# Channel shuffle: the tiles at both ends of a load-copy-store pipeline become larger

## The chip, the cores and the metric

One core of one Trainium2 chip runs the kernel. The metric is the time of one execution on the device in microseconds (us), taken as the median of several runs. A profile, recorded in one execution, is read beside it.

A few words that recur: VectorE (DVE in the profile) is the engine that copies here. SP and ACT are the engines whose sequencers issue transfers; the work of a transfer is done by 16 DMA engines that the core has. The on-chip memory has 128 partitions, and "38 KB a partition" means 128 rows of 38 KB.

## The reference

The input is a tensor of 16 x 64 x 64 x 256 values in float32, 67.11 MB. Its 256 channels are seen as 8 groups of 32, and the two are swapped: channel `g*32 + j` goes to place `j*8 + g`.

```python
def reference(x, groups):
    batch, h, w, c = x.shape
    channels_per_group = c // groups
    x = x.reshape(batch, h, w, groups, channels_per_group)
    x = x.transpose(0, 1, 2, 4, 3)
    x = x.reshape(batch, h, w, c)
    return x.astype(np.float32)
```

No arithmetic is done. Every byte is read once and written once.

## The kernel before

There are 65,536 pixels of 256 channels (1 KB each), 512 pixels for each partition. The list `_SLOTS` cuts these 512 into tiles, in order: the numbers are pixels, and so KB, a partition. A tile of several numbers is loaded, copied and stored in so many parts. Before, the list is a tile in two parts (4 and 8), one of 28, twelve of 38 and one of 16.

The loop over `_SLOTS` (L45) takes a load buffer (`in_tile`, L46) and a store buffer (`out_tile`, L47). Both have the size of the largest tile, 38 KB a partition; there are two load buffers and three store buffers, used in turn. For each part of a tile it issues three things:

- a load on SP's queue (L55): DRAM to `in_tile`. A part is one contiguous block of DRAM; each partition gets one contiguous row of it.
- a copy on VectorE (L57): `in_tile` to `out_tile`, and this copy carries out the shuffle through its access pattern.
- a store on ACT's queue (L61): `out_tile` to DRAM, again one contiguous row for a partition.

What orders the work: instructions on one engine run in the order in which they are written. A load into a buffer waits until the copy of the tile two places earlier is done. A copy waits for its load and, from the fourth tile on, for the store of the tile three places earlier. A store waits for its copy. SP issues nothing but loads and ACT nothing but stores, so neither holds the other up. No scheduler reorders anything (`manual_schedule`).

Transfers of one issuing engine are worked off in order by the DMA engines. Loads and stores are separate queues on the same 16 DMA engines.

Of the kernel before, what the change touches and what calls it, by code (L numbers as in the profile page):

```python
# [1 line left out]

# [4 lines left out]


F32 = mybir.dt.float32
P = 128  # L10

_SLOTS = [[4, 8], [28]] + [[38]] * 12 + [[16]]
_IN_BUFS = 2
_OUT_BUFS = 3


@with_exitstack
def kernel(
    ctx: ExitStack,
    tc: tile.TileContext,  # L20
    x: bass.AP,
    groups: bass.AP,
    out: bass.AP,
):
    nc = tc.nc
    b, h, w, c = x.shape
    G = int(groups)
    CPG = c // G
    assert G * CPG == c
    assert sum(map(sum, _SLOTS)) * P == b * h * w  # L30
    biggest = max(map(sum, _SLOTS))

    x_flat = x.rearrange("b h w c -> (b h w c)")
    out_flat = out.rearrange("b h w c -> (b h w c)")

    in_pool = ctx.enter_context(tc.tile_pool(name="in_pool", bufs=_IN_BUFS))
    out_pool = ctx.enter_context(tc.tile_pool(name="out_pool", bufs=_OUT_BUFS))

    def rows(flat, first, q):

        return flat[first * c : (first + P * q) * c].rearrange("(p f) -> p f", p=P)

    ctx.enter_context(tc.manual_schedule(engines=None))
    first = 0
    for parts in _SLOTS:  # L45
        in_tile = in_pool.tile([P, biggest * c], F32, name="in_tile")  # L46
        out_tile = out_pool.tile([P, biggest * c], F32, name="out_tile")  # L47
        at = 0
        pieces = []
        for q in parts:  # L50
            pieces.append((q, first, slice(at * c, (at + q) * c)))
            first += P * q
            at += q
        for q, start, cols in pieces:
            nc.sync.dma_start(out=in_tile[:, cols], in_=rows(x_flat, start, q))  # L55
        for q, start, cols in pieces:
            nc.vector.tensor_copy(  # L57
                out=out_tile[:, cols].rearrange("p (i j g) -> p i j g", j=CPG, g=G),
                in_=in_tile[:, cols].rearrange("p (i g j) -> p i j g", g=G, j=CPG),
            )  # L60
            nc.scalar.dma_start(  # L61
                out=rows(out_flat, start, q), in_=out_tile[:, cols]
            )


# [1 line left out]
_INS = ['x', 'groups']  # L67
_OUTS = [((16, 64, 64, 256), 'float32')]

_NUMBERS = {'groups': 8}  # L70


# [26 lines left out]
```

## Time and profile before

| what | value |
|---|---|
| time, median of 3 runs | 316.34 us (316.31 to 316.68) |
| span of the profiled execution, first to last instruction | 314.4 us |
| what lies between the span and the median | 1.9 us |
| DMA traffic | 67.11 MB read, 67.11 MB written |
| mean rate over the span | 427 GB/s |
| load of 38 KB a partition, issue to landing (median of 12) | 37.0 us |
| store of 38 KB a partition, issue to landing (median of 12) | 42.6 us |
| last load (16 KB), issue to landing | 30.4 us |
| last store (16 KB), issue to landing | 15.2 us |
| first store (4 KB), issue to landing | 14.3 us |

The profile gives no time of its own for the profiled execution beyond its span; the sums are made against the span, and the rest up to the median is taken as it stands.

How to read it: the page begins with the span and the busy time of each engine. "DMA queues" then lists packets, bytes and the share that the packets took of the time of all 16 DMA engines; a share of 50% in a window of 100 us means 800 us of packet time, spread over 16 engines. The queue view can be asked for any window; it counts the packets that start inside it, so a short window can show more than 100%. The load queue is q1, the store queue q10. In a group line such as those of the copies, the columns are: line, engine, operation, output and input, their shapes, the count; then busy us and the mean ns of one; then the idle time of the engine before them and what ended it. In a timeline line the first two numbers are start and duration in us.

### The profile page before, as it was taken

The numbers are of one execution on the slowest core, as the hardware profiler recorded it, in microseconds if no ns is written. First come the engines' busy times: TensorE is split into PE (matmuls) and PEld (weight loads), VectorE is DVE, ScalarE is ACT, GpSimd is POOL, SyncE is SP. The second block draws the span as 40 slices with busy tenths as digits, with TensorE's granted clock in tenths as the row PEclk, the third lists the DMA queues.
The fourth block names the chain that finished last, engine by engine and source line by source line (L and its number), as shares of the span: only waits on it lengthen the run. The fifth ranks groups of instructions, "written<-read, shape, count | busy, mean of one in ns | idle before, by whom it ended". The sixth has DMA issues, their size and how long they took to land.

```text
span 314.4 us, 132 instructions
## 1 busy us (share of the span) xinstructions
DVE 119.0 (38%) x16; POOL 0.2 (0%) x4
## 2 busy tenths in 40 slices
DVE  2081907309109109019028028037046055065400
POOL 0000000000000000000000000000000000000000
DMA  7999999999999999999999999999999999999997
GB/s 317 405 441 416 435 416 483 401 465 406 450 421 446 426 436 436 401 470 396 475 396 475 396 470 401 470 401 470 401 450 421 446 426 436 436 417 450 429 421 321
DMA packets 4608, 134.22 MB, mean 427 GB/s; under 512 B 512, under 2 KB 512, under 8 KB 768
## 3 DMA queue, kind: packets, MB, share of 16 engines
q1 hardware_dynamic: 2304, 67.11, 49.8%
q10 hardware_dynamic: 2304, 67.11, 49.4%
HBM read 67.11 MB, written 67.11 MB: 427 GB/s over the span
## 4 chain that ended last, share of the span: by engine, by line
DMA 76%; DVE 19%; issue 0%; SPq 0%; DVEq 0%
DMA in_tile<-in_x_dram 76%; DVE out_tile L57 19%; SPq L55 0%; DVEq L57 0%
## 5 line engine op out<-in xcount | busy, mean ns | idle before, releaser
L57 DVE COPY out_tile<-in_tile 128x9728 f32<-128x9728 f32 (+4 forms) x16 | 119.0, 7440 | 179.4 <-DMA in_tile<-in_x_dram 179.4
L80 POOL MEMSET const-uint8-127<- 128x1 uint8 x1 | 0.1, 103 | 0.0
L80 POOL MEMSET const-bfloat16-1.0<- 128x1 bf16 x1 | 0.1, 102 | 0.0
L80 POOL MEMSET const-float32-1.0<- 128x1 f32 x1 | 0.1, 100 | 0.0
L80 POOL MEMSET const-float32-0.0<- 128x1 f32 x1 | 0.1, 99 | 0.2 <-issue 0.2
## 6 DMA issues: line engine op xcount, KB each, us to landing
in_tile<-in_x_dram SPq DMA_DIRECT2D x12, 4864.0 KB, 37.0
out_dram<-out_tile ACTq DMA_DIRECT2D x12, 4864.0 KB, 42.6
in_tile<-in_x_dram SPq DMA_DIRECT2D x1, 3584.0 KB, 14.7
out_dram<-out_tile ACTq DMA_DIRECT2D x1, 3584.0 KB, 30.9
in_tile<-in_x_dram SPq DMA_DIRECT2D x1, 2048.0 KB, 30.4
out_dram<-out_tile ACTq DMA_DIRECT2D x1, 2048.0 KB, 15.2
in_tile<-in_x_dram SPq DMA_DIRECT2D x1, 1024.0 KB, 5.4
out_dram<-out_tile ACTq DMA_DIRECT2D x1, 1024.0 KB, 25.0
```

The source lines that it names most:

```text
L57: nc.vector.tensor_copy(out=out_tile[:, cols].rearrange("p (i j g) -> p i j g", j=CPG, g=G), in_=in_tile[:, cols].rearrange("p (i g j) -> ...
L80: nc = _bacc.Bacc("TRN2", target_bir_lowering=False, num_devices=1)
```

## The change

One line changes. The tile in two parts (4 and 8 KB) and the tile of 28 KB at the beginning give way to one tile of 24 KB; the twelve tiles of 38 KB stay; the last tile grows from 16 to 32 KB. There are 14 tiles in place of 15, each in one part, so 14 loads, copies and stores in place of 16. The two load buffers and three store buffers and their sizes stay, as does all other code.

```diff
-_SLOTS = [[4, 8], [28]] + [[38]] * 12 + [[16]]
+_SLOTS = [[24]] + [[38]] * 12 + [[32]]
 _IN_BUFS = 2
 _OUT_BUFS = 3
```

## The prediction

> **What bounds the kernel now.** I read the page first, then the DMA view in short windows, then copies by shape, the timeline and the chain of waits. The page's head:
>
> ```profile
> span 314.4 us, 132 instructions
> DVE 119.0 (38%) x16; POOL 0.2 (0%) x4
> ...
> q1 hardware_dynamic: 2304, 67.11, 49.8%
> q10 hardware_dynamic: 2304, 67.11, 49.4%
> ```
>
> q1 carries the loads, q10 the stores. Their packets fill 99.2% of the 16 DMA engines' span; VectorE works 38% of it. The chain's 76% for loads and 19% for copies is only the order in which work ended; while VectorE sat in that chain the DMA engines were busy with stores. So the limit is DMA time, and an edit can change the end in three ways: less DMA time, a hole in it, or another start or finish.
>
> A transfer has 2304/16 = 144 packets, so 9 for each engine: 8 rows and one packet that reports completion. How the queues share an engine, from windows 80 to 264 us and 9.11 to 17.73:
>
> ```profile
> q10 hardware_dynamic: 1152, 39.85, 50.1%
> q1 hardware_dynamic: 1152, 39.85, 50.1%
> ```
>
> ```profile
> q1 hardware_dynamic: 128, 3.54, 96.3%
> q10 hardware_dynamic: 128, 0.52, 14.8%
> ```
>
> Both windows have equal counts, although in the second a store row is 4 KB and most load rows 28 KB. The queues take turns packet by packet; bytes don't count. A row's time is share x 16 x window / rows. 38 KB: 0.501 x 16 x 184 / 1024 = 1.440 us. 4 KB: 0.148 x 16 x 8.62 / 128 = 0.159. In the same way 8 KB takes 0.309 (20.25 to 31.86, 21.3%), 28 KB 1.063 (34.6 to 52.17, 48.4%) and 16 KB 0.611 (278.7 to 292.7, 34.9%).
>
> **The DMA time that the change removes and adds.** Removed: rows of 4, 8, 28 and 16 KB, 8 an engine, once in each queue: 8 x (0.159 + 0.309 + 1.063 + 0.611) = 17.14 us. Added: 24 and 32 KB rows. No row has them; between their neighbours, 0.611 + 8/12 x 0.452 = 0.912 and 1.063 + 4/10 x 0.377 = 1.214; 8 x 2.126 = 17.01. The difference, 0.13 a queue, is **-0.26 us** for two. The bounds are the best and worst bytes per second of those rows: at the 4 KB row's rate the 56 KB take 8 x 14 x 0.159 = 17.81 a queue (+1.3 for both), at the 38 KB row's 8 x 56/38 x 1.440 = 16.98 (-0.3). I keep -0.26, since both new sizes lie between rows that run near the 38 KB rate. The other twelve tiles and all bytes stay.
>
> The Trainium skill, page "DMA: Bandwidth & Descriptors", section "Anatomy of one DMA — SWDGE (gpsimd) path", counts a fixed cost of about 2.0 us for each transfer, beside the bytes. Four transfers fewer would by that rule (an estimate) save 8 us, for some 308. The packet times above contradict it for queued transfers, and I don't use it in the sum.
>
> **Issue and copy work.** Two DMA issues fewer on SP (0.33 us each) and on ACT (0.36): hidden now by rows in flight, worth nothing; without that cover they would be a gain of 2 x 0.33 + 2 x 0.36 = 1.4. VectorE loses copies of 1.09, 2.02, 6.57 and 3.87 and gains two; between the rows below, 24 KB (6144 elements) takes 3.87 + 2/3 x 2.70 = 5.67 and 32 KB (8192) 6.57 + 0.4 x 2.22 = 7.46. In total -0.4 us on an engine that idles 179, so nothing, except at the two ends.
>
> ```profile
> L57 DVE COPY out_tile<-in_tile 128x9728 f32<-128x9728 f32 x12 | 105.5, 8791 | 158.5 <-DMA in_tile<-in_x_dram 158.5
> L57 DVE COPY out_tile<-in_tile 128x7168 f32<-128x7168 f32 x1 | 6.6, 6569 | 7.7 <-DMA in_tile<-in_x_dram 7.7
> L57 DVE COPY out_tile<-in_tile 128x4096 f32<-128x4096 f32 x1 | 3.9, 3873 | 7.6 <-DMA in_tile<-in_x_dram 7.6
> ```
>
> **The start.** The first load is issued at 0.73; no packet starts before 1.74, and the windows after it are full. Both kernels have this lead of 1.02 us. The load that completes the first 12 KB landed at 6.59 = 1.75 + 8 x (0.159 + 0.309) + 1.10. So the 24 KB tile lands at 1.75 + 7.30 + 1.10 = 10.15 (the 4 KB one landed at 4.0), its copy ends at 15.84 and its store is issued at 15.87 instead of 5.19. That later first store costs nothing as long as loads fill the engines: the 38 KB load is queued behind the 24 KB one and lasts until about 9.8 + 8 x 1.44 = 21.3, and the third load is issued at 15.84. If it were not there, the cost would be the wait from 9.8 to the store.
>
> What the later store does change is how many load turns run ahead of the first store turn; call it the lead. Before, the store issued at 5.19 had its first packet at about 9.12 (the q10 rows of the window from 9.11 on). Between 6.3 and 9.11 the engines started only loads:
>
> ```profile
> q1 hardware_dynamic: 32, 0.92, 80.3%
> ```
>
> That is two 28 KB rows an engine (0.92 MB / 32), after one that began by 6.3. So the lead was 9 + 9 + 3 = 21 turns. I read it as: the store arrives 1.1 to 1.75 us after its issue, during the first 28 KB row, and two packets are already taken ahead of it. After the change the arrival is at 17.0 to 17.6. The 38 KB rows start at 9.8 + 1.44 k, so the sixth is then running (from 17.0), and two more go ahead: lead 9 + 8 = 17. If the arrival catches the fifth, or if the 3.93 us are plain delay (15.87 + 3.93 = 19.8, when seven rows are through), it is 16. I take 17 and keep 16 for the range.
>
> In the middle a lead of 17 is enough. When a load lands, 17 - 9 = 8 store turns are still queued, which alternate with loads and last about 8 x 2.88 = 23 us, against a copy of 8.8. The output buffers wait on a store three tiles back, long done; no new wait arises.
>
> **The end, where cover is thin.** After the last load nothing but queued stores keeps the DMA engines busy until the last copy is stored. Before: 144 load turns, lead 21, so 123 store turns done of the 135 up to the last 38 KB store: 12 left, of which 10 are rows, 14.4 us. The window 294.42 to 308.42, from that landing on, bears this out:
>
> ```profile
> q10 hardware_dynamic: 192, 5.87, 97.0%
> ```
>
> 192/16 = 12 packets. The last copy and store fit into it easily:
>
> ```profile
> 294.54 3.87 DVE L57 COPY out_tile<-in_tile 128x4096 f32<-128x4096 f32 x1 [7.62 <-DMA in_tile<-in_x_dram]
> ```
>
> After: 126 load turns, lead 17, 109 store turns done of 117: 8 left, 7 of them rows, **10.08 us** of cover. Needed: last row to landing 0.35 (the last store's rows end at 313.28, it lands at 298.45 + 15.2), 0.12 to the copy (294.42 to 294.54), 7.46 of copy, 0.03 to the issue, then the way to the first store packet. The trace shows no store to idle engines. The nearest row is the first load, 1.02; the other end is the first store's 3.93, rows in front of it included. I take 1.02: the need is 8.98 and 1.1 us remain. Cost of the tail: 0. With lead 16 the cover is 6 x 1.44 = 8.64 and a hole of 0.34 opens, 1.07 if the way takes 1.75.
>
> The same rule of the page (about 2.0 us, mostly the receipt) speaks against the change here, since at the tail nothing hides it. With 2.0 for the 0.35 and 1.02 the need would be 9.61: still covered with lead 17, a hole of 0.97 with 16 (an estimate from that page).
>
> **Sum.** 314.4 - 0.26 = 314.2 for the span. The three runs before have median 316.34, so 1.9 us lie around the span; I leave these as they are. 316.34 - 0.26 = **316.1 us**. A measurement of this kernel can tell about 0.2% (0.63 us) from no change, so this is no change.
>
> **Rivals.** (1) A short hole: lead 16 with 1.02 to 1.75 to the packet. 316.1 + 0.34 to 1.07 = 316.4 to 317.2. For it: the fifth row ends just where the arrival may fall. Against: before, all 16 engines agreed on three rows, which puts the arrival past 1.1 us.
> (2) Slower: the last store, issued at the tail, needs its 3.93 us even on idle engines. Need 11.89, hole 1.81 (lead 17) to 3.25 (lead 16): 317.9 to 319.3. It decides from a way of 10.08 - 7.96 = 2.1 us on. For it: that is the only store start in the trace. Against: whole 28 KB rows passed in that time, 3.2 us of it, so queued packets explain it.
> (3) Faster: the small rows cost more than their packet time. Packets ran from 1.75 to 313.28, 311.5 us; all 512 KB a partition and queue at the 38 KB rate need 16 x 512/38 x 1.440 = 310.4. If all of that 1.1 came from small tiles, 315.2. Against: much of it is the stream's start, which stays.
>
> **Chances.** Forecast 0.53, (1) 0.23, (2) 0.15, (3) 0.07, a loss of another kind 0.02. Over 0.2% faster: (3) and 0.01 of the forecast's edge, 0.08. Slower: (2), the rest 0.02, and 0.07 of (1) that lies above 317.0, 0.24. Same: 0.68. The forecast's own range is 315.9 to 316.4. The range to be held takes in (1), some of (3) and the foot of (2): 315.6 to 317.8.
>
> **What would show it.** Both queues' shares still near 99%, first packet near 1.75, first copy starting near 10.2, first store packet after eight 38 KB load rows an engine, last landing of a load near 295 with 7 rows of 38 KB left, and packets without a break to the end. Wrong: a stretch near 303.5 in which no packet starts, or row times off the line for 24 or 32 KB.

## The result and the profile after

The changed kernel takes 317.15 us in the median of 11 runs, the kernel before 316.31 us in 11 runs beside them. The ratio is 1.0029, with a 95% interval of 1.002 to 1.0039: 0.3% slower. Three of the eleven executions took 331.5 to 334.2 us and are left out of the ratio; none of the 11 of the kernel before did. The prediction was 316.1 us and no change. The measured time lies inside the range that was given (315.6 to 317.8), but on the other side of no change from the forecast's small gain.

The profiled execution took 316.71 us, the shortest of the eleven. The head of its page:

```profile
span 314.9 us, 121 instructions
DVE 119.5 (38%) x14; POOL 0.2 (0%) x4
...
q1 hardware_dynamic: 2016, 67.11, 49.8%
q10 hardware_dynamic: 2016, 67.11, 49.3%
```

99.1% against 99.2%: the DMA engines are as full as before, and the span is still 0.5 us longer. The difference sits in four places.

**The start.** The DMA view of the changed kernel from 1.72 to 9.63 us holds the 128 rows of the first tile:

```profile
q1 hardware_dynamic: 128, 3.15, 100.2%
```

1.002 x 16 x 7.91 / 128 = 0.991 us a row. Later rows of 24 KB take 0.912 (the store window 22.2 to 38.7: 44.2% x 16 x 16.5 / 128), as predicted. So the start costs 8 x 0.079 = 0.63 us beyond the rows. The first copy, which waits for this tile, starts at 10.73:

```profile
10.73 5.72 DVE L57 COPY out_tile<-in_tile 128x6144 f32<-128x6144 f32 x1 [10.73 <-DMA in_tile<-in_x_dram]
```

Before, the window 1.74 to 5.88 was filled in this way:

```profile
q1 hardware_dynamic: 270, 1.56, 97.9%
```

That is 4.05 us an engine. Of the 270 packets 16 report completion and 254 are rows (128 of 4 KB, 126 of 8 KB), worth 3.71: 0.34 lost.

**The row ahead of the first store.** From 19.8 to 22.2 us the 16 engines of the changed kernel start one row each, the last of the first 38 KB load:

```profile
q1 hardware_dynamic: 16, 0.62, 100.6%
```

1.006 x 16 x 2.4 / 16 = 2.41 us for a row that takes 1.44 elsewhere: 0.97 us lost on every engine, and the first store row comes behind it. Before, two rows show the same, the one ahead of the first store (7.99 to 9.1) and one before the 28 KB store began (32.9 to 34.6):

```profile
q1 hardware_dynamic: 16, 0.46, 106.0%
```

```profile
q1 hardware_dynamic: 15, 0.58, 98.8%
```

1.060 x 16 x 1.11 / 16 = 1.18 for a row of 1.063 is 0.11 lost, and 0.988 x 16 x 1.7 / 15 = 1.79 against 1.44 is 0.35. Smaller lengthenings stand between these two in the kernel before, 0.10 in 9.11 to 17.73 (96.3% is 132.8 us over 16 engines, for rows worth 131.2) and, in the same way, 0.14 in 20.25 to 31.86. Together 0.70. The stretches beside these windows hold 0.11 more (5.88 to 7.99, 17.73 to 20.25, 31.86 to 32.9), and 9.63 to 19.8 in the changed kernel holds 0.04: 0.81 before, 1.01 after.

**The tail.** After the last load lands, at 294.24 us, the stores of the changed kernel run on, in the windows 294.24 to 303.5 and 303.5 to 313.2:

```profile
q10 hardware_dynamic: 96, 3.74, 93.2%
```

```profile
q10 hardware_dynamic: 146, 4.19, 100.2%
```

Six 38 KB rows an engine start after the landing and a seventh is running, and then the 32 KB rows follow without a break. The last copy ends in time:

```profile
294.32 7.55 DVE L57 COPY out_tile<-in_tile 128x8192 f32<-128x8192 f32 x1 [12.27 <-DMA in_tile<-in_x_dram]
```

Its store is issued at 301.89 and the first of its rows starts at about 303.5, behind the rows of the store before. No hole opened at the tail in this execution.

**After the last landing.** SP's waits at the end of the program, for the kernel before and then for the changed one (us in total, times, longest):

```profile
SPq L94 <- DMA out_dram<-out_tile: 49.1, 3, 33.0
```

```profile
SPq L94 <- DMA out_dram<-out_tile: 54.3, 1, 54.3
```

The final waits check the completion semaphores of the transfers two at a time, in a fixed order. Before, the one that came last was the last to be checked. With 14 transfers in place of 16, the last store's semaphore is in the first pair, and three more checks of about 0.065 us follow when it has come. From the last landing to the end of the program 0.985 us pass in place of 0.813: 0.17 more.

**The sum of it:** row time -0.26, start +0.29, rows ahead of the stores +0.20, final waits +0.17: +0.40. The spans differ by 0.5. About 0.1 us is not assigned; a lengthened row can overlap the start of the next, so no single term is surer than that.

### The profile page after: what moved, and what is told of

Read it like the earlier page. It is cut to its first block, busy times and chain, and to the rows that moved or that the text cites. A ratio compares the mean times of both kernels' runs of the same rounds, so it can differ in the third digit from the quotient of the medians.

```text
span 314.9 us, 121 instructions
## 1 busy us (share of the span) xinstructions
DVE 119.5 (38%) x14; POOL 0.2 (0%) x4
## 4 chain that ended last, share of the span: by engine, by line
DMA 76%; DVE 19%; issue 0%; SPq 0%; DVEq 0%
DMA in_tile<-in_x_dram 76%; DVE out_tile L57 19%; SPq L55 0%; DVEq L57 0%
## 5 line engine op out<-in xcount | busy, mean ns | idle before, releaser
L57 DVE COPY out_tile<-in_tile 128x9728 f32<-128x9728 f32 (+2 forms) x14 | 119.5, 8536 | 182.4 <-DMA in_tile<-in_x_dram 182.4
```

Of the source, the lines that this page charges most:

```text
L57: nc.vector.tensor_copy(out=out_tile[:, cols].rearrange("p (i j g) -> p i j g", j=CPG, g=G), in_=in_tile[:, cols].rearrange("p (i g j) -> ...
```

## The experiments

Each run is compared with runs of the kernel before on the same chip, 316.1 to 316.2 us in the median. STORE, HEAD, QUEUE, TAIL, START and COUNT are names of theories; where one was changed by a result, the next expectation has it in its new form. Each is put into words in the expectation that names it first.

**again.** The changed kernel without an edit.

> The changed kernel once more, for a second profiled execution. Both theories: a median near 317.1 us. Theory HEAD (the loss of 0.8 us is at the start: the first 24 KB rows start slowly, and near 20 us the last 38 KB load row ahead of the first store is stretched by about 1.0 us): these two stretches are in this profile too, with the same sizes, and the rows of the last 38 KB store run into those of the 32 KB store without a break. Theory TAIL (most executions have a hole ahead of the last store, which the first profile, of a fast execution, happened not to have): when this profile's span is longer than 314.9 us, the difference is a stretch near 303.5 us in which no packet starts.

317.40 us, ratio 1.0033 (1.0021 to 1.0046): the loss repeats. The profiled execution took 334.8 us: in it one engine falls up to 13 us behind the others, so it does not decide between HEAD and TAIL, which stayed with the next run.

**tail_halves.** The last tile in two copies and two stores, columns 0 to 16 KB and 16 to 32 KB of the same rows. In this form of the list the first sizes of a tile are those of its loads, the second those of its copies and stores.

```diff
-_SLOTS = [[24]] + [[38]] * 12 + [[32]]
+_SLOTS = [([24], [24])] + [([38], [38])] * 12 + [([32], [16, 16])]
```

> The last 32 KB tile is loaded as before but copied and stored in two halves of 16 KB a partition, so the first of its stores is issued about 3.6 us earlier and no hole can open at the tail. HEAD: 317.0 to 317.3 us, as the changed kernel, since the start is untouched and two extra row turns cost 0.1. TAIL: 316.4 to 316.7, the hole of the median execution is gone.

Ratio 1.0032 (1.0019 to 1.0045), no gain: the typical loss isn't a hole at the tail. The profiled execution took 317.11 us, close to the median of the change, and its span is 315.3, 0.9 over the kernel before. Its start, from 1.72 to 9.62:

```profile
q1 hardware_dynamic: 126, 3.10, 102.4%
```

1.027 us a row, so 0.92 over the plain 8 rows, 0.58 more than before. With -0.2 for the rows, +0.2 for the rows ahead of the stores and +0.19 for the final waits (1.007 us from the last landing to the end) that gives about +0.8 of the 0.9. This suggests that a median execution of the changed kernel differs from its shortest mostly by the start; no profile of the unedited kernel at its median shows it.

**head_parts.** The first 24 KB as blocks of 4, 8 and 12, each loaded, copied and stored by itself.

```diff
-_SLOTS = [[24]] + [[38]] * 12 + [[32]]
+_SLOTS = [[4, 8, 12]] + [[38]] * 12 + [[32]]
```

> The first 24 KB tile in parts of 4, 8 and 12 KB, each loaded, copied and stored by itself; the 32 KB tile at the end stays whole. HEAD: 316.0 to 316.4 us, no stretched row of 1 us near 20 us, the first rows after the start as in the kernel before. TAIL: the earlier store takes part of the lead or adds to it; with a lead of 21 turns or more the cover is 14 us and the time is also 316.0 to 316.4. So this run tells whether the loss hangs on the head at all; if it stays above 316.9, both theories are wrong about the head.

317.16 us (316.43 to 317.85), ratio 1.0031 (1.0019 to 1.0043). A miss: the small blocks alone do not restore the time. In the profiled execution (317.85) the DMA engines fell out of step. In the profiles of the kernel before, the changed kernel and tail_halves, the 16 engines complete a load within 0.2 to 0.9 us of each other; here they are up to 3.4 us apart, and the last engine ends at 314.91 while the others end by 313.34. The kernel before ended at 313.28, so the loss of this execution is one engine's lag. No row near 20 us is longer by 1 us.

**head_loads.** The 24 KB tile loaded as columns of 4, 8 and 12 KB, copied and stored whole.

```diff
-_SLOTS = [[24]] + [[38]] * 12 + [[32]]
+_SLOTS = [([4, 8, 12], [24])] + [([38], [38])] * 12 + [([32], [32])]
```

> The first 24 KB tile is loaded in parts of 4, 8 and 12 KB (columns of the same rows), but copied and stored whole, as in the changed kernel. Only the size of the first rows changes; the first store is as late as in the changed kernel. HEAD by the slow first rows: 316.7 to 316.9 us, 0.3 less, with the stretch near 20 us still there. HEAD by the late first store: 317.1, unchanged. TAIL: 317.1, since the lead stays 17 turns, or a little less if the 24 KB tile lands earlier.

318.62 us, ratio 1.0066 (1.0048 to 1.0084): slower still, which neither form of HEAD had. The start lost as much as with 24 KB rows (0.78 us), although the rows were 4 and 8 KB wide, and the long row stayed. The engines were 2 to 3.5 us apart, and between 303.4 and 305.7 us a hole of 1.8 us an engine stands ahead of the last store.

**early_third.** The first tile is loaded into a store buffer, so that the third load need not wait for the first copy.

```diff
-        in_tile = in_pool.tile([P, biggest * c], F32, name="in_tile")
+        pool = in_pool if first else out_pool
+        in_tile = pool.tile([P, biggest * c], F32, name="in_tile" if first else "out_tile")
```

> The first 24 KB tile is loaded into a store buffer (the third store buffer is free until the third copy), so the third load is no longer behind the first copy and is issued right after the start. Theory QUEUE (the load queue of the changed kernel runs empty near 20 us: the third load is issued at 16.5, its first row comes 4 to 5 us later, and the last row queued ahead of it ends at 21.3; the 16 engines then start stores in different turns and one of them lags to the end): no stretched row near 20 us, all engines in step, and 316.0 to 316.5 us. Theory STORE (the stretch is the price of the first store's start, whatever the load queue holds): a load row ahead of the first store is still stretched by about 1 us, 316.8 to 317.3 us. Theory TAIL: the lead is 17 turns as before, so the hole of the slower executions stays, 316.8 to 317.3.

318.54 us, ratio 1.0067 (1.0052 to 1.0082). QUEUE falls: with the third load queued from 1.6 us on, the rows ahead of the first store are still 1.07 us longer. TAIL's hole, too, is real in some kernels. Here the last load lands at 297.04, and in the window 303 to 304.6 the engines are nearly empty:

```profile
q10 hardware_dynamic: 16, 0.12, 17.3%
```

**second_12.** The head of the kernel before, with a second tile of 12 in place of 28 KB.

```diff
-_SLOTS = [[4, 8], [28]] + [[38]] * 12 + [[16]]
+_SLOTS = [[4, 8], [12]] + [[38]] * 12 + [[32]]
```

> The head of the kernel before with a short second tile: 4 and 8 KB, then 12 KB, twelve of 38, 32 at the end. The third load is issued near 8.7 us, as in the kernel before, but the rows queued ahead of it end near 10 us and not near 16. QUEUE: its first row comes 4 to 5 us after issue, near 13; the small first store fills 1.3 us of that, so about 2 us of DMA time are lost near 10 to 13 us, 317.8 to 319. If the way from issue to first packet is 1.02 us as the prediction took it, nothing is lost: 316.0 to 316.4. STORE: the first store starts with a small row, so 316.1 to 316.5.

328.09 us, ratio 1.0378 (1.0365 to 1.0391), far outside every expectation. Nothing of 10 us is lost at the head. The whole run is in another rhythm; the window from 80 to 264 us:

```profile
q10 hardware_dynamic: 1104, 37.98, 52.7%
q1 hardware_dynamic: 1099, 37.78, 47.5%
```

Without the completion packets that is 0.527 x 2944 / 976 = 1.59 us for a 38 KB store row, against 1.44 in the kernel before. Each load lands within 0.2 us of the store issued with it, and a tile takes about 24.2 us in place of 23.0.

**first_38.** The widest tile first.

```diff
-_SLOTS = [[24]] + [[38]] * 12 + [[32]]
+_SLOTS = [[38]] * 13 + [[18]]
```

> Thirteen tiles of 38 KB, then 18 KB. The first copy ends near 24 us and the two loads' rows end near 26, so 2 us lie between the third load's issue and the end of the queued rows, against 4.8 in the changed kernel. The tail is a small tile with long cover. QUEUE: a loss of 2 to 3 us near 26 us, more than in the changed kernel: 318 to 319.3. STORE: one row stretched by about 1 to 1.5 us: 317.0 to 317.6. TAIL: no loss, 316.0 to 316.4, since the last copy takes 4.2 us.

332.28 us, ratio 1.0491 (1.0465 to 1.0516). The row ahead of the first store lost 1.54 us, as STORE expected, but the same slow rhythm follows it and decides the time (store rows 52.7% in the same window).

**first_18.** 18 KB first, 38 KB last, the last in two copies and stores of 19 KB.

```diff
-_SLOTS = [[24]] + [[38]] * 12 + [[32]]
+_SLOTS = [([18], [18])] + [([38], [38])] * 12 + [([38], [19, 19])]
```

> 18 KB first, thirteen tiles of 38 KB, the last of them copied and stored in two halves so that the tail is covered. The third load is issued near 13 us and the rows ahead of it end near 19.6: 6.6 us. QUEUE: no loss near 20 us, engines in step, 316.1 to 316.6. STORE: a stretched row of about 0.7 us is still there, 316.7 to 317.2. TAIL: 316.1 to 316.5.

322.16 us, ratio 1.0188 (1.0175 to 1.0201). The rows ahead of the first store lost 0.9 us, for a store row of 18 KB. The rest of the loss comes from the edit at the tail, by the copies' shapes:

```profile
L60 DVE COPY out_tile<-in_tile 128x4864 f32<-128x4864 f32 x2 | 16.7, 8408 | 14.1 <-DMA in_tile<-in_x_dram 14.1
L60 DVE COPY out_tile<-in_tile 128x4608 f32<-128x4608 f32 x1 | 4.3, 4328 | 9.8 <-DMA in_tile<-in_x_dram 9.8
```

A copy of 19 pixels a partition takes nearly twice as long as one of 18, so each half came late and left a hole (302 to 304.3 and 310.2 to 312.6 us). The run's time says nothing about the head alone.

**tail_only.** The tail of the change with the head of the kernel before.

```diff
-_SLOTS = [[4, 8], [28]] + [[38]] * 12 + [[16]]
+_SLOTS = [[4, 8], [28]] + [[38]] * 11 + [[22], [32]]
```

> The tail of the change alone: 4, 8 and 28 KB at the head as in the kernel before, eleven tiles of 38 KB, 22 KB, and 32 KB last (one tile of 38 KB gives way to the 22, to keep the sum). STORE: 316.0 to 316.4 us, as the kernel before. TAIL: 316.8 to 317.3, as the whole change.

316.14 us, ratio 0.9999 (0.999 to 1.0007). A last tile of 32 KB costs nothing behind the old head. With the old head there are also 16 transfers again, and 0.81 us from the last landing to the end.

**head_only.** The head of the change, with 16 KB last.

```diff
-_SLOTS = [[24]] + [[38]] * 12 + [[32]]
+_SLOTS = [[24]] + [[38]] * 12 + [[16], [16]]
```

> The head of the change alone: 24 KB first, twelve tiles of 38 KB, and at the end two tiles of 16 KB, so that the last one is the 16 KB tile of the kernel before. Theory STORE (the loss is at the head: the first store begins after a long stretch of loads alone, and its first row is not read ahead, so all engines lose about the time of one such row, 0.9 to 1.1 us for 24 KB, where the 4 KB row of the kernel before lost 0.2): 316.9 to 317.4 us, as the whole change. TAIL: 316.0 to 316.4.

319.59 us, ratio 1.0085 (1.0065 to 1.0105), more than either theory expected. The first part is as STORE had it: the rows ahead of the first store are 1.17 us longer. The rest is a hole, from 308 to 311 us:

```profile
q10 hardware_dynamic: 27, 0.18, 14.3%
```

The second 16 KB load has to wait for a load buffer and lands at 307.0, after the queued stores have run out. This is the cover of the prediction's tail, used up by a tile more at the end, so the run isn't the clean half that it was meant to be. tail_only is.

**first_store_4.** One copy of 24 KB, then its store as columns of 4 and 20 KB; the second sizes cut the stores alone here.

```diff
-_SLOTS = [[24]] + [[38]] * 12 + [[32]]
+_SLOTS = [([24], [4, 20])] + [([38], [38])] * 12 + [([32], [32])]
```

> The changed kernel, but the store of the first tile goes out as two transfers, rows of 4 KB and then of 20 KB, both after the one copy of 24 KB; loads and copies are untouched and the first store is as late as before. STORE: the stretch near 20 us falls from 1.0 to about 0.2 us, the time to 316.2 to 316.5. If it is the lateness of the first store or the empty load queue that costs, and not the size of its first row, the stretch stays at 1.0 us and the time at 316.9 to 317.4. (The small rows also let the loads run further ahead, which would show at the tail as longer cover; in the rows, that is told apart from the stretch.)

317.24 us, ratio 1.0029 (1.0019 to 1.004): no gain, but the profile shows why. Ahead of the first store, at 19.6 to 21.29 us, nothing is lost any more; at 32.3 to 34.85, ahead of the 20 KB rows, the loss stands again:

```profile
q1 hardware_dynamic: 16, 0.62, 85.5%
...
q1 hardware_dynamic: 16, 0.62, 95.3%
```

0.855 x 16 x 1.69 / 16 = 1.44 us a row, the plain time, and 0.953 x 16 x 2.55 / 16 = 2.43, 0.99 more. So what costs here is not the first store as such but the first wide store row behind narrow ones, even with loads queued and the store issued long before. STORE had the wrong place for it.

**late_parts.** Blocks of 4, 8 and 12 KB as in head_parts, but one copy for all 24, and the three stores after it.

```diff
-        for q, start, cols in pieces:
-            nc.vector.tensor_copy(...)
-            nc.scalar.dma_start(...)
+        nc.vector.tensor_copy(...)
+        for q, start, cols in pieces:
+            nc.scalar.dma_start(...)
```

> The first 24 KB in blocks of 4, 8 and 12 KB a partition, loaded and stored as three transfers each, but copied at once, so that the first store is as late as in the changed kernel, and there are 16 transfers in each direction again. Theory START (the first rows of the program cost more when they are wide or far apart in memory: 0.6 to 0.9 us over the plain row time with a first tile of 24 KB, 0.15 to 0.45 with blocks of 4 KB): the start loses 0.15 to 0.45 as in the kernel before. Theory COUNT (the last store of 14 falls on a completion semaphore that the final waits look at first, three more waits of 0.065 us follow; of 16 it is the last one looked at): last landing to end 1.16 - 0.35 = 0.81 us and not 0.99. Both together, without a price for lateness: 316.1 to 316.6 us. If the lateness of the first store costs in itself: 316.9 to 317.4.

316.45 us in the median of 12, against 316.17 for the kernel before. The ratio, 1.0027 (1.0008 to 1.0046), does not tell it from the changed kernel; three executions of 317.8 to 319.8 raise and widen it. Eight were within 316.27 to 316.83. The first store is issued at 16.21, as late as in the change: in these eight, lateness itself costs little or nothing. The start, from 1.73 to 5.9, is 99.8% full, 4.16 us for rows worth 3.71, so 0.45. Last landing to end takes 0.81 us again, as COUNT expected, with 16 transfers.

The run also narrows what first_store_4 said. Its store rows grow from 4 to 8, 12 and 38 KB. Ahead of the 4 KB rows 0.25 us is lost (18.2 to 19.9), but ahead of the first 38 KB store rows, from 60.4 to 62.1, almost nothing:

```profile
q1 hardware_dynamic: 16, 0.62, 87.7%
```

0.877 x 16 x 1.7 / 16 = 1.49 against 1.44. A wide store row alone does not lengthen the row ahead of it by 1 us; it did so where no store row, or only rows of 4 KB, had gone before.

**before_pitch.** The kernel before, its first tile one block of 12 KB rows, of which the transfers take columns.

```diff
-            pieces.append((q, first, slice(at * c, (at + q) * c)))
+            pieces.append((sum(parts), first, slice(at * c, (at + q) * c)))
...
-rows(x_flat, start, q)
+rows(x_flat, start, q)[:, cols]
```

> The kernel before, except that its first tile of 4 and 8 KB is one block of 12 KB rows in DRAM, of which the two loads and stores take columns; row sizes, order and count stay. START by distance (rows further apart): 0.1 to 0.4 us more at the start, 316.3 to 316.6. START by row width alone: 316.0 to 316.3, as the kernel before.

316.63 us in the median of 11 (316.10 to 317.36), ratio 1.001 (1.0001 to 1.002). The first two loads landed 0.7 us later (7.30 against 6.59) with the same row widths. Distance between rows is enough to slow the start; that width alone would too isn't shown. The time followed in part, with a wide spread, and the profiled execution is one of the longest (317.15).

## Why the prediction was wrong

- **What bounds the kernel** was right: DMA time, 99% full before and after, rows in turns. So were the new row times: 0.912 predicted and 0.912 measured for 24 KB; for 32 KB, 1.214 predicted, and the last eight rows fill 303.5 to 313.2, 9.7 us, 1.21 each.
- **The start** failed. "So the 24 KB tile lands at 1.75 + 7.30 + 1.10 = 10.15" took the remainder of the kernel before over as it stood. It landed at 10.70, and just before 10.98 in tail_halves. The term that was left out is a loss at the first rows, 0.34 before and 0.63 to 0.92 with the 24 KB tile. head_loads and before_pitch show it with small rows that lie far apart, late_parts half of it with small blocks. The prediction also let the 38 KB rows start at 9.8, though by its own sum the 24 KB rows end at 1.75 + 7.30 = 9.05; they started from 9.63 on. That lost time was thus in its count of turns but not in its price.
- **"That later first store costs nothing as long as loads fill the engines"** failed. Loads did fill them, in early_third even with a third load queued from the start, yet the row ahead of the first store row was 0.97 us longer (1.07 in early_third). The prediction had noted no such row in the kernel before, though 0.11 and 0.35 could be read there in the same way. In late_parts a store as late cost 0.25 there; first_store_4 moves the 1 us to the first wide row behind narrow ones. The net of this term is +0.20.
- **"I leave these as they are"**, said of what lies around the DMA time, missed the final waits: +0.17, by the number of transfers. late_parts, with 16, has the old value.
- **The tail** was right for this kernel. The lead came out at 17 turns, seven rows were left, and the store needed less than the 1.6 us it had. tail_halves gains nothing by an earlier store, and tail_only loses nothing. The way from issue to first packet, taken as 1.02 from the first load, is 0.84 where the store queue had run empty (early_third, issued at 304.68, first row at 305.52; the same in head_loads and head_only). So the slower rival, 3.93 us even on idle engines, falls. So does the need of 9.61 with a fixed 2.0 us: the end of the last row to its landing took 0.33, which with 0.84 makes 1.2 (that rule's heading puts it on the gpsimd path, and these transfers are issued by SP and ACT). A hole ahead of the last store, as the first rival had it, does occur in early_third, head_loads and head_only, where the last load lands later.
- **The sum** was -0.26 where the spans differ by +0.5 in the shortest execution; the measured terms make +0.40 of it. That the time still fell inside the range is luck as far as the mechanism goes: the range was held for holes at the tail, and none of these opened.

What stays open: why the row ahead of the first wide store row is lengthened (0.9 us for 18 KB, 0.97 for 24, 1.54 for 38, but 0.35 for 28 after 8, 0.99 for 20 after 4 and 0.05 for 38 after 12, so its own row time doesn't set it alone), why the first rows of the program cost more, and what lets the engines fall out of step in some executions. No version here beats the kernel before; tail_only equals it.

## What to carry to other kernels

This pipeline already fills its DMA engines, and what the change lost sat at the two ends, in tenths of a microsecond each: read the first transfers row by row, not by their total bytes, and look for rows that take longer than the same row later. Behind the head of the kernel before the engines stayed within 0.5 us of each other, in tail_only too; behind most other heads they did not, small blocks included (head_parts), and edits of the head moved the time by up to 5%, while the tail alone could be changed for nothing. Count the waits after the last transfer too: which completion is checked last is part of the time.

## What was not expected of the hardware

- A kernel can settle in a lasting slower rhythm: store rows of 38 KB at 1.59 us in place of 1.44 for the whole run, with nothing different in the middle of the program, only at its ends (second_12 and first_38, +3.8% and +4.9%). There each load lands within 0.2 us of the store issued with it, where the kernel before has them 5.7 us apart and the changed one 3. In again the landings fall together from 92 us on and a tile then takes 24.3 to 25 us, though most rows keep their 1.44. What comes first, the pace or the landings, is open.
- A VectorE copy of 19 x 256 values took 8.41 us and one of 18 x 256 took 4.33.
- Two loads of 4 and 8 KB rows landed 0.7 us later when their rows were 12 KB apart in DRAM than when they lay dense.
- The order of the final waits over completion semaphores was worth 0.17 us.
- A store issued to an empty store queue had its first packet 0.84 us later, in early_third, head_loads and head_only alike.
